# Low parts of forty weight units: an accumulating DMA in place of GpSimd's subtraction

## The chip, the cores and the metric

The kernel runs on one core of one Trainium2 chip. The metric is the device time of one execution in microseconds. Three runs of the kernel before took 841.36, 841.49 and 846.52 us; their median is 841.49.

The engines are named as the profile names them: PE is TensorE (PEld its weight loads), DVE is VectorE, ACT is ScalarE, POOL is GpSimd, SP is SyncE, which here only starts DMAs.

## The reference

Two layers of a decoder trunk work on 512 prompt rows and 8 sample rows of 1024 channels with shared weights. Layer 0 mixes two convolutions, layer 1 a gated unit over chunks of 128 rows. Cut to what matters here:

```python
def ab_mixer(x, ...):                       # layer 0
    z = x @ w_in                            # 1024 -> 7 x 1024
    a_val, a_gate, b_post, c_pre, h, g = split(z)
    a = causal_dwconv31(a_val * sigmoid(a_gate)) + bias
    a = silu(layer_norm(a))
    s = causal_dwconv3(c_pre * h)
    y = concat([a, b_post * s]) * silu(g)
    return y @ w_out                        # 2048 -> 1024

def c_mixer(x, ...):                        # layer 1
    u, v, g = split(x @ w_in)               # 1024 -> 3 x 2048
    u, v = gelu(u), layer_norm(gelu(v))
    mix = tril(w_s) @ v + b_s               # per chunk of 128 rows and head
    return (u * mix * silu(g)) @ w_out

x = layer_norm(alpha * x + mixer(x))        # after each layer
```

Everything is float32. The convolution states and the sample rows' v are outputs too.

## The kernel before

**Products in two parts.** The 520 rows are columns of every product, in two halves of 260; channels lie on the 128 partitions. The weights come as 136 units, numbered 0 to 135 in the order of their use. A unit holds 1024 input channels times 128 output channels, as a tile of 128 x 8 x 128 values (512 KB). TensorE multiplies in the type float32r, which keeps fewer bits than float32. So a weight tile `raw` is split into a high part `whi`, which is `raw` rounded to float32r, and a low part `wlo = raw - whi`; the rows are split likewise (`xh`, `xl`). A product is whi·xh + wlo·xh + whi·xl: 3 matmuls for each of 8 channel blocks and 2 halves, 48 to a unit (`mm2`).

**Where the parts come from.** `load_unit` (lines 116 to 125) does four things for unit n: SyncE starts the load into `raw` (3 buffers), ScalarE writes the high part by a cast (line 121), and the engine that `ON_POOL` (line 127) names subtracts for the low part (line 124): GpSimd for units 4 to 45 and 66 to 83, VectorE for the other 74. High and low parts lie in a ring of 12 tiles, so six units are there at a time and a unit's tiles can be filled once the unit six places ahead of it has been used. Units 0 and 1 are split in a start-up loop of their own. A unit is asked for `LEAD` = 5 units ahead.

**Layer 0.** Units 0 to 31 come in rounds of four for each of 8 channel blocks i: gate, value, c and h. ScalarE takes the sigmoid of the gate (`sg`), VectorE multiplies it with the value from PSUM (`apad`, line 306); ScalarE copies c, VectorE multiplies it with h from PSUM (`ch`, line 325). Two PSUM tiles (`zt`) serve these products in turn, so that a product can begin only when the one before the last has been emptied by ScalarE or VectorE. On VectorE also run the convolution of width 3 (`sB`, line 332, two steps a block) and that of width 31: 30 steps `acc` a block with the accumulator in PSUM (line 269), two blocks in turn, put in at low priority wherever the scheduler sees VectorE free. The sample rows' convolutions are `proda`, `cas`, `prodb`, `sbs`. Then come the units 32 to 39 (`z_post`, multiplied into sB by VectorE, line 392), 40 to 47 (gate of B), 48 to 55 (first half of the output projection), 56 to 63 (gate of A), and 64 to 71 (second half of the output projection, in two row halves, `out_part`), each followed by a layer norm over the channels whose steps are mostly VectorE's.

**Layer 1.** Units 72 to 87 give v, then u, gate and output projection in two rounds to unit 135.

**What sets the order.** Each engine works through its own queue in order. A scheduler with a model of the engines' times places the instructions in these queues when the kernel is built; so each engine's order is fixed in the program, and an instruction that waits holds all that stand behind it on its engine.

Of the kernel before, what the change touches and what calls it, by code (L numbers as in the profile page):

```python
# [9 lines left out]
F32 = mybir.dt.float32  # L10
# [3 lines left out]
ALU = mybir.AluOpType  # L14
# [3 lines left out]
D = 1024  # L18
# [12 lines left out]
ALPHA = 4.0 ** 0.25  # L31
EPS = 1e-5

# columns of the packed per-channel parameters
PA_W = 0
PA_B = 31
PA_G = 32
# [13 lines left out]
def decoder_kernel(  # L51
# [19 lines left out]
    nc = tc.nc  # L71
# [10 lines left out]
    def xs_slot(dt, name):  # L82
        return slots.tile([P, T], dt, tag="X", name=name, bufs=16)
# [25 lines left out]
    def hs(h):  # L109
        return slice(h * TH, (h + 1) * TH)  # L110

# [1 line left out]
    n_units = 2 + wu.shape[0]  # L113
    units = [None, None]

    def load_unit(wtag=("W", 12)):
        n = len(units)
        raw = wpool.tile([P, KT, P], F32, tag="raw", name=f"raw_{n}", bufs=3)
        nc.sync.dma_start(raw, wu[n - 2])
        hi = wpool.tile([P, KT, P], F32R, tag=wtag[0], name=f"whi_{n}", bufs=wtag[1])  # L120
        nc.scalar.copy(hi, raw)  # L121
        lo = wpool.tile([P, KT, P], F32R, tag=wtag[0], name=f"wlo_{n}", bufs=wtag[1])
        eng = nc.gpsimd if n in ON_POOL else nc.vector
        eng.tensor_tensor(lo, raw, hi.bitcast(F32), op=ALU.subtract)  # L124
        units.append((hi, lo))

    ON_POOL = set(range(4, 46)) | set(range(66, 84))
    EXTRA = set()
    for base in (64, 128):
        EXTRA.update((base + 6, base + 7))  # L130
# [31 lines left out]
                        stop=(k == KT - 1 and j == 2),  # L162
                    )

    # products of a constant until the first rows are there, so that the array's clock is up by then
    warm = const.tile([P, P], BF16, name="warm")
    nc.vector.memset(warm, 1.0)
    wps = mt("warm")
    for j in range(NWARM):
        nc.tensor.matmul(wps[:, :P], warm, warm, start=True, stop=True)  # L170

    # the input rows come with the first two weight units, one k tile after the other, and the
    # products follow in that order
    xh, xl = [], []
    w0h, w0l = [], []
    zg = zt("z_first")
# [2 lines left out]
    for k in range(KT):  # L179
        x = tmp(f"x_{k}")  # L180
        if k % 4 == 0:
            raw = wpool.tile([P, 4, 2, P], F32, tag="raw", name=f"raw_s{k}", bufs=3)
# [4 lines left out]
        cuts = 2 if k == 0 else 1  # L187
# [3 lines left out]
        h = xs_slot(F32R, f"xh_{k}")  # L191
        lo = xs_slot(F32R, f"xl_{k}")
# [22 lines left out]
    load_unit()  # L215
    pa = const.tile([P, KT, NPA], F32, name="pa")
    nc.sync.dma_start(pa, pa_in)
    # powers of two, so float32r holds them as well
    ones_r = const.tile([P, P], F32R, name="ones_r")
    ones_d = ones_r.bitcast(F32)  # L220
    nc.gpsimd.memset(ones_d, 1.0 / D)
# [6 lines left out]
    neg_half = const.tile([P, NS], F32, name="neg_half")  # L228
    nc.gpsimd.memset(neg_half, -0.5)

    # ================= layer 0 =================
    unit(1)
    xs = []
    for j in range(2):
        t = wpool.tile([P, 4, NS, WA], F32, tag="M", name=f"xs_{j}", bufs=4)
# [46 lines left out]
    n = 0  # L282
    for i in range(KT):
# [44 lines left out]
        s = slots.tile([P, T], F32, tag="SB", name=f"sB_{i}", bufs=8)  # L328
# [9 lines left out]
                op1=ALU.add,  # L338
            )

    # the sample rows of both convolutions
    nc.gpsimd.dma_start(cbs_out, xb)
    prodb = btmp("prodb")[:, : KT * NS * WB].rearrange("p (a b c) -> p a b c", a=KT, b=NS)
    nc.vector.tensor_tensor(
# [3 lines left out]
        op=ALU.mult,  # L348
# [5 lines left out]
    with background():  # L354
        for j in range(2):
# [6 lines left out]
                op=ALU.mult,  # L362
# [5 lines left out]
                    cA[i][:, SEQ:], cas[:, i - 4 * j, :], AF.Identity, bias=pa[:, i, PA_B : PA_B + 1]  # L368
                )

    # layer norm of the wide convolution over the channels, then silu
    def mean_of(m, src, name):
        """the sum of src / D over the channels, from its two float32r parts"""
        both = tpool.tile([P, T], F32R, tag="B", name=f"parts_{name}", bufs=4)
        nn = src.shape[-1]
        hi, lo = both[:, :nn], both[:, TH : TH + nn]
        nc.scalar.copy(hi, src)
        nc.vector.tensor_tensor(lo, src, hi.bitcast(F32), op=ALU.subtract)
        nc.tensor.matmul(m, ones_r, hi, start=True, stop=False)
        nc.tensor.matmul(m, ones_r, lo, start=False, stop=True)  # L380
# [11 lines left out]
        nc.vector.tensor_tensor(two(sB[i]), zh(z), two(sB[i]), op=ALU.mult)  # L392

    def split_y(i, g, other, tag, parts):
        """y = g * other as its two parts, in that many cuts of the rows"""
        h = y_slot(F32R, f"yh_{tag}{i}")
        lo = y_slot(F32R, f"yl_{tag}{i}")
        for j in range(parts):
            c = slice(j * T // parts, (j + 1) * T // parts)
            nc.vector.tensor_tensor(g[:, c], g[:, c], other[:, c], op=ALU.mult)  # L400
            nc.scalar.copy(h[:, c], g[:, c])
            nc.vector.tensor_tensor(lo[:, c], g[:, c], h[:, c].bitcast(F32), op=ALU.subtract)
        yh.append(h)
        yl.append(lo)
# [66 lines left out]
    gated(cA, "a")  # L471

    def out_part(base, c0, c1, yh, yl, res, lnc, done, last=False, pool_sub=()):
        """The second half of an output projection for the rows c0..c1, the residual, and the layer
        norm over the channels. The sums of the norm are of the rows less the mean of their first
        512 channels, so that no large mean cancels in the variance."""
        c = slice(c0, c1)
        nn = c1 - c0
        key = f"{base}_{c0}"
# [92 lines left out]
    def split_x1(d, c0, c1):  # L572
# [10 lines left out]
    out_part(n, TH, T, yh, yl, res, LN0_G, split_x1)()  # L583
    n += KT

    # ================= layer 1 =================
    wt = wpool.tile([P, NH, P], F32, tag="M", name="wt", bufs=4)
    nc.gpsimd.dma_start(wt, wsT_in)
    bs = wpool.tile([P, NH, P], F32, tag="M", name="bs", bufs=4)
    nc.gpsimd.dma_start(bs, bs_in)  # L590
    # wt[s, h, t] is kept where s <= t
    nc.gpsimd.affine_select(
        wt, wt, pattern=[[0, NH], [1, P]], compare_op=ALU.is_ge, fill=0.0, base=0, channel_multiplier=-1
    )
    # and its float32r parts, for the column sums
    wth, wtl = [], []
    for j in range(2):
        w = wt[:, 4 * j : 4 * j + 4, :].rearrange("p a b -> p (a b)")
# [29 lines left out]
    for i in range(NVF):  # L628
        z = one(i, f"z_v{i}_1")[:, :TH]
        mm(z, unit(n + i), x1h, x1l, hs(1))  # L630
        t = vt[i]
# [18 lines left out]
    def v_finish():  # L650
        v_tok(NV - 1)
        for c in range(NC):
            nc.vector.bn_aggr(mv[:, c, :], stats[:, c, :, :].rearrange("p a b -> p (a b)"))
        nc.vector.tensor_scalar_add(rs, mv[:, :, 1], EPS)
        nc.gpsimd.tensor_tensor(rs, rs, neg_half[:, :NC], op=ALU.pow)
        for i in range(NV):
            for c in range(NC):
                nc.vector.tensor_scalar(
                    vtok[i][:, c * P : (c + 1) * P],
                    vtok[i][:, c * P : (c + 1) * P],  # L660
                    mv[:, c, 0:1],
                    rs[:, c : c + 1],
                    op0=ALU.subtract,
                    op1=ALU.mult,
                )
        # column sums of the causal weights, for the shift of the norm
        for j in range(2):
            m = mt(f"rows_{j}")
            nc.tensor.matmul(m, ones_r, wth[j], start=True, stop=False)
            nc.tensor.matmul(m, ones_r, wtl[j], start=False, stop=True)  # L670
            nc.scalar.mul(
                rowsum[:, 4 * j : 4 * j + 4, :].rearrange("p a b -> p (a b)"), m, float(D)
            )
        # the sample rows' layer norm
        ssum = tiny.tile([P, NS], F32, name="ssum")
        nc.vector.tensor_reduce(ssum, vs.rearrange("p a b -> p b a"), axis=AX.X, op=ALU.add)
        m = mt("vs_mean")
        nc.tensor.matmul(m[:, :NS], ones_d, ssum, start=True, stop=True)
        smean = tiny.tile([P, NS], F32, name="smean")
        nc.vector.tensor_scalar_mul(smean, m[:, :NS], 0.5)  # L680
        bc = lambda t: t[:, None, :].to_broadcast([P, NV, NS])
        nc.vector.tensor_tensor(vs, vs, bc(smean), op=ALU.subtract)
        vq = mixs
        nc.vector.tensor_tensor(vq, vs, vs, op=ALU.mult)
        qsum = tiny.tile([P, NS], F32, name="qsum")
        nc.vector.tensor_reduce(qsum, vq.rearrange("p a b -> p b a"), axis=AX.X, op=ALU.add)
        m = mt("vs_var")
        nc.tensor.matmul(m[:, :NS], ones_d, qsum, start=True, stop=True)
        srs = tiny.tile([P, NS], F32, name="srs")
        nc.vector.tensor_scalar(srs, m[:, :NS], 0.5, EPS, op0=ALU.mult, op1=ALU.add)  # L690
        nc.gpsimd.tensor_tensor(srs, srs, neg_half, op=ALU.pow)
        nc.vector.tensor_tensor(vs, vs, bc(srs), op=ALU.mult)
        pb = lambda j: pv[:, :, j : j + 1].to_broadcast([P, NV, NS])
        nc.vector.tensor_tensor(vs, vs, pb(0), op=ALU.mult)
        nc.vector.tensor_tensor(vs, vs, pb(1), op=ALU.add)
        nc.gpsimd.dma_start(vs_out, vs)
        four = lambda t: t.rearrange("p (a c) b -> p a c b", c=2)
        nc.vector.tensor_tensor(
            four(mixs), four(vs), ws00[:, :, None, None].to_broadcast([P, NH, 2, NS]), op=ALU.mult
        )  # L700
        nc.vector.tensor_tensor(
            four(mixs), four(mixs), bs[:, :, None, 0:1].to_broadcast([P, NH, 2, NS]), op=ALU.add
        )
# [83 lines left out]


def _units(w, e0, e1):
    """[1024, e] columns e0..e1 as [n, 128 (k inside), 8 (k tile), 128]"""  # L790
    w = w[:, e0:e1]
    n = (e1 - e0) // P
    return w.reshape(KT, P, n, P).transpose(2, 1, 0, 3)


def _chan(a, n):
    """[..., n*128] -> [128, n, ...]"""
    a = a.reshape(a.shape[:-1] + (n, P))
    k = a.ndim
    return a.transpose((k - 1, k - 2) + tuple(range(k - 2)))  # L800
# [86 lines left out]
```

## Time and profile before

| | |
|---|---|
| runs | 841.36, 841.49, 846.52 us |
| profiled execution: span from its first to its last instruction | 840.8 us (its own time isn't listed beside it; the median lies 0.7 above the span) |
| mean granted TensorE clock | 0.991 |
| PE, DVE, ACT, POOL busy | 97%, 66%, 37%, 23% |
| GpSimd's subtractions for low parts | 60, 145.6 us |
| VectorE's subtractions for low parts | 74, 90.2 us |
| ScalarE's casts for high parts | 134, 140.0 us |
| read from HBM, written to it | 77.91 MB, 3.44 MB |

A busy share is an average over stages. VectorE is busy in nearly all of the first 250 us and less than two thirds of the time behind it; GpSimd's subtractions lie before 210 us and between 340 and 470 us. TensorE's matmuls overlap, so the count of matmuls in a stage tells more of its pace than its busy time: in an undisturbed stretch there are 355 in 42 us.

### The profile page before, as it was taken

The numbers are of one execution on the slowest core, as the hardware profiler recorded it, in microseconds if no ns is written. First come the engines' busy times: TensorE is split into PE (matmuls) and PEld (weight loads), VectorE is DVE, ScalarE is ACT, GpSimd is POOL, SyncE is SP. The second block draws the span as 40 slices with busy tenths as digits, with TensorE's granted clock in tenths as the row PEclk, the third lists the DMA queues.
The fourth block names the chain that finished last, engine by engine and source line by source line (L and its number), as shares of the span: only waits on it lengthen the run. The fifth ranks groups of instructions, "written<-read, shape, count | busy, mean of one in ns | idle before, by whom it ended". The sixth has DMA issues, their size and how long they took to land.

```text
span 840.8 us, 15982 instructions
## 1 busy us (share of the span) xinstructions
PE 816.4 (97%) x6792; PEld 813.8 (97%) x6792; DVE 557.8 (66%) x894; ACT 309.5 (37%) x470; POOL 193.7 (23%) x178
## 2 busy tenths in 40 slices
PE   9989999998999999999999999999999999999994
PEld 8989999998999999999999999999999999999993
DVE  5899999999994487356696333495455433625566
ACT  5423322333124346333466533333432133333243
POOL 0844355544340000024252711101000000000022
PEclk9999999999999999999999999999999999999998
DMA  8533333223223452424050522204223233222011
GB/s 301 164 103 101 101 103 102 96 82 130 72 79 101 122 166 66 126 76 126 26 166 12 171 81 82 95 24 156 77 76 95 82 101 94 83 79 99 1 51 51
DMA packets 27110, 82.38 MB, mean 98 GB/s; under 512 B 3568, under 2 KB 7296, under 8 KB 27040
## 3 DMA queue, kind: packets, MB, share of 16 engines
q1 hardware_dynamic: 26000, 79.01, 30.1%
q0 software_dynamic: 1040, 2.36, 0.7%
q8 instruction: 53, 0.87, 0.4%
q14 instruction: 17, 0.14, 0.1%
HBM read 77.91 MB, written 3.44 MB: 97 GB/s over the span
## 4 chain that ended last, share of the span: by engine, by line
PE 71%; DVE 23%; DMA 2%; issue 2%; ACT 1%; SPq 0%; POOL 0%; ACTq 0%; DVEq 0%; POOLq 0%
DVE acc L269 14%; PE z_gc L157 11%; PE z_u L157 11%; PE z_p L141 9%; PE z_v L157 7%; PE z_q L157 5%; PE z_o L157 5%; PE z_gb L157 5%; PE z_ga L157 5%; PE z_post L157 4%; PE z_v L141 4%; DVE sB L332 3%; DMA raw<-in_wu 2%; PE mix L713 2%; PE vt L615 1%
## 5 line engine op out<-in xcount | busy, mean ns | idle before, releaser
L121 ACT CAST whi<-raw 128x1024 fp32r<-128x1024 f32 x134 | 140.0, 1047 | 300.6 <-issue 66.6
L124 POOL TENSOR_TENSOR wlo<-raw,whi 128x1024 fp32r<-128x1024 f32 x60 | 145.6, 2434 | 262.6 <-ACT whi L121 262.3
L124 DVE TENSOR_TENSOR wlo<-raw,whi 128x1024 fp32r<-128x1024 f32 x74 | 90.2, 1222 | 131.0 <-ACT whi L121 131.0
L269 DVE SCALAR_TENSOR_TENSOR acc<-apad,pa,acc 128x512 f32<-128x512 f32 x240 | 166.6, 748 | 2.5 <-ACT acc L266 0.8
L157 PE MATMUL z_gc<-x1h,whi 128*128 128x260 f32 x256 | 72.9, 285 | 0.0
L157 PE MATMUL z_u<-x1h,whi 128*128 128x260 f32 x256 | 72.4, 283 | 0.0
L157 PE MATMUL z_gc<-x1h,wlo 128*128 128x260 f32 x256 | 72.0, 281 | 0.0
L157 PE MATMUL z_u<-x1l,whi 128*128 128x260 f32 x256 | 72.0, 281 | 0.0
L157 PE MATMUL z_gc<-x1l,whi 128*128 128x260 f32 x256 | 72.0, 281 | 0.0
L157 PE MATMUL z_u<-x1h,wlo 128*128 128x260 f32 x256 | 72.0, 281 | 0.0
L157 PEld LDWEIGHTS z_u<-x1h,wlo 128*128 128x128 f32 x256 | 48.1, 188 | 0.1
L157 PEld LDWEIGHTS z_gc<-x1h,wlo 128*128 128x128 f32 x256 | 48.2, 188 | 0.0
L157 PEld LDWEIGHTS z_u<-x1h,whi 128*128 128x128 f32 x256 | 48.1, 188 | 0.1
L157 PEld LDWEIGHTS z_gc<-x1l,whi 128*128 128x128 f32 x256 | 48.1, 188 | 0.0
L157 PEld LDWEIGHTS z_u<-x1l,whi 128*128 128x128 f32 x256 | 48.1, 188 | 0.0
L157 PEld LDWEIGHTS z_gc<-x1h,whi 128*128 128x128 f32 x256 | 48.1, 188 | 0.0
L725 POOL COPY mix<-mixs 128x8 f32<-128x8 f32 x16 | 3.5, 226 | 186.5 <-DVE gu L752 174.1
L157 PE MATMUL z_v<-x1h,whi 128*128 128x260 f32 x160 | 46.0, 287 | 0.0
L157 PE MATMUL z_v<-x1h,wlo 128*128 128x260 f32 x160 | 45.0, 281 | 0.0
L157 PE MATMUL z_v<-x1l,whi 128*128 128x260 f32 x160 | 44.9, 281 | 0.0
L157 PE MATMUL z_post<-xh,whi 128*128 128x260 f32 x128 | 36.8, 288 | 4.2 <-DVE sB L392 4.2
L157 PE MATMUL z_h<-xh,whi 128*128 128x260 f32 x128 | 36.9, 288 | 4.0 <-DVE apad L306 4.0
(259 smaller groups left out, 2758.5 us busy)
## 6 DMA issues: line engine op xcount, KB each, us to landing
raw<-in_wu SPq DMA_DIRECT2D x134, 512.0 KB, 3.6
xr<-in_xT SPq DMA_DIRECT2D x8, 260.0 KB, 4.6
x<-in_xT SPq DMA_DIRECT2D x7, 260.0 KB, 4.4
out_y<-r SPq DMA_DIRECT2D x8, 130.0 KB, 1.8
out_y<-out SPq DMA_DIRECT2D x4, 260.0 KB, 2.2
raw_s<-in_w SPq DMA_DIRECT2D x8, 128.0 KB, 4.2
xs<-in_cache_a SPq DMA_DIRECT2D x2, 496.0 KB, 9.2
out_cas<-xs POOLq DMA_DIRECT2D x2, 496.0 KB, 4.5
```

The source lines that it names most:

```text
L121: nc.scalar.copy(hi, raw)
L124: eng.tensor_tensor(lo, raw, hi.bitcast(F32), op=ALU.subtract)
L141: nc.tensor.matmul(ps, a[:, k, :], b[k][:, c], start=(k == 0 and j == 0), stop=(k == KT - 1 and j == 2),)
L157: nc.tensor.matmul(z[h][:, :TH], a[:, k, :], b[k][:, hs(h)], start=(k == 0 and j == 0), stop=(k == KT - 1 and j == 2),)
L269: nc.vector.scalar_tensor_tensor(acc[i], apads[i][:, j : j + SEQ], pa[:, i, PA_W + j : PA_W + j + 1], acc[i], op0=ALU.mult, op1=ALU.add,)
L332: nc.vector.scalar_tensor_tensor(s[:, :SEQ], ch[:, j : j + SEQ], pa[:, i, PB_W + j : PB_W + j + 1], s[:, :SEQ], op0=ALU.mult, op1=ALU.add,)
L615: nc.tensor.transpose(m[:, c * P : (c + 1) * P], vt[i][:, c * P : (c + 1) * P], ident)
L713: nc.tensor.matmul(m[:, c * P : (c + 1) * P], vtok[i][:, c * P : (c + 1) * P], wt[:, h, :], start=True, stop=True)
L725: nc.gpsimd.tensor_copy(t[:, SEQ:], mixs[:, i, :])
```

## The change

Units 10 to 49 get their low parts in another way. ScalarE, behind the cast for the high part, also writes `-raw` into the low part's tile, which is of the type float32r and so holds the negated high part. Then GpSimd starts a DMA that reads the same unit from HBM a second time and adds it to the tile in place: `-whi + raw`. GpSimd subtracts for no unit any more. Units 4 to 9 and 66 to 83, which it had besides, go to VectorE; units 46 to 49, which were VectorE's, are made by DMA. VectorE so makes the low parts of 94 loaded units in place of 74, and 40 DMAs of 512 KB are added, which read 21 MB more. Some comments go as well, which does nothing.

```diff
@@ load_unit
         hi = wpool.tile([P, KT, P], F32R, tag=wtag[0], name=f"whi_{n}", bufs=wtag[1])
         nc.scalar.copy(hi, raw)
         lo = wpool.tile([P, KT, P], F32R, tag=wtag[0], name=f"wlo_{n}", bufs=wtag[1])
-        eng = nc.gpsimd if n in ON_POOL else nc.vector
-        eng.tensor_tensor(lo, raw, hi.bitcast(F32), op=ALU.subtract)
+        if n in BY_DMA:
+
+            nc.scalar.mul(lo, raw, -1.0)
+            nc.gpsimd.dma_start(lo, wu[n - 2], accum_op=ALU.add)
+        else:
+            nc.vector.tensor_tensor(lo, raw, hi.bitcast(F32), op=ALU.subtract)
         units.append((hi, lo))
 
-    ON_POOL = set(range(4, 46)) | set(range(66, 84))
+
+    BY_DMA = set(range(10, 50))
     EXTRA = set()
```

## The prediction

> **What bounds the kernel now.** I read the page's busy shares first, then who waited for whom on TensorE, then the span cut into stages, then single instructions where TensorE stood still.
>
> The first line is from the page (busy us, share, instructions); the five below it are TensorE's waits (us in total, times, longest).
>
> ```profile
> PE 816.4 (97%) x6792; PEld 813.8 (97%) x6792; DVE 557.8 (66%) x894; ACT 309.5 (37%) x470; POOL 193.7 (23%) x178
> ...
> PE z_post L157 <- DVE sB L392: 4.2, 1, 4.2
> PE z_h L157 <- DVE apad L306: 4.0, 1, 4.0
> PE warm L170 <- DVE warm L167: 1.1, 1, 1.1
> PE shift L497 <- DVE tot L492: 0.8, 1, 0.8
> ...
> PE z_gate L157 <- ACT c L317: 0.6, 1, 0.6
> ```
>
> TensorE sets the time. The largest holes are two waits for VectorE, which must empty a PSUM tile before the next product may use it. The stages show the holes as missing matmuls (the number after x, first column group), with the granted clock (PEclk) beside them.
>
> ```profile
> 42.00:63.00 21.00, 17.00 (x130) 16.80 (x129) 20.72 (x29) 4.98 (x6) 10.03 (x8) 0.92 0.35 103
> 63.00:84.00 21.00, 21.00 (x179) 21.00 (x179) 20.75 (x28) 6.52 (x8) 9.56 (x6) 1.00 0.32 102
> 84.00:105.00 21.00, 20.36 (x172) 20.16 (x171) 20.93 (x26) 7.01 (x12) 8.22 (x9) 1.00 0.33 101
> 189.00:210.00 21.00, 18.77 (x158) 18.57 (x157) 20.96 (x29) 6.70 (x16) 9.83 (x9) 1.00 0.39 130
> 210.00:252.00 42.00, 40.02 (x325) 40.02 (x326) 40.38 (x52) 8.99 (x15) 16.88 (x7) 0.96 0.23 76
> 252.00:294.00 42.00, 42.00 (x355) 42.00 (x355) 18.28 (x22) 17.59 (x24) 0.00 (x0) 1.00 0.36 110
> 386.00:430.00 44.00, 42.48 (x349) 41.94 (x348) 32.93 (x62) 17.83 (x32) 15.26 (x7) 1.00 0.30 90
> ```
>
> A full stretch gives 355 matmuls in 42 us, 8.45 per us. Against that, 42–63 lacks 48, or 5.7 us; 84–105 lacks 6, or 0.7; 189–210 lacks 20, or 2.4; 210–252 lacks 30, or 3.5; 386–430 lacks 23, or 2.7. Each of the two waits of 4 us costs about 1.7 us more, since the clock is lower after it (0.08 of 21 us; 0.04 of 42). So 15.0 us can be had between the start and the tail, and no more: the floor is about 826.
>
> VectorE is late there because single instructions of it run long. The rows are VectorE's and GpSimd's timeline (start, duration), then four groups (count | busy us, mean ns), then two ranges (min/median/max ns).
>
> ```profile
> 36.37 7.68 DVE L332 SCALAR_TENSOR_TENSOR sB<-ch,pa,sB 128x512 f32<-128x512 f32 x1
> 36.37 7.13 POOL L124 TENSOR_TENSOR wlo<-raw,whi 128x1024 fp32r<-128x1024 f32 x3
> ...
> L332 DVE SCALAR_TENSOR_TENSOR sB<-ch,pa,sB 128x512 f32<-128x512 f32 x16 | 29.3, 1831 | 0.9 <-ACT sB L330 0.9
> L358 DVE TENSOR_TENSOR proda<-xs,pa 128x992 f32<-128x992 f32 x2 | 6.5, 3273 | 0.0
> L124 DVE TENSOR_TENSOR wlo<-raw,whi 128x1024 fp32r<-128x1024 f32 x74 | 90.2, 1222 | 131.0 <-ACT whi L121 131.0
> L124 POOL TENSOR_TENSOR wlo<-raw,whi 128x1024 fp32r<-128x1024 f32 x60 | 145.6, 2434 | 262.6 <-ACT whi L121 262.3
> ...
> L332 DVE SCALAR_TENSOR_TENSOR sB<-ch,pa,sB x16: 739/1154/7678, 33.4 to 207.1; 128x512 f32<-128x512 f32 x16
> L269 DVE SCALAR_TENSOR_TENSOR acc<-apad,pa,acc x240: 737/747/757, 23.4 to 247.5; 128x512 f32<-128x512 f32 x120
> ```
>
> The sB instruction that takes 0.74 us at best took 7.68 us and ended 0.55 us after three GpSimd subtractions of 7.13 us that began with it. The 240 conv steps, whose accumulator lies in PSUM, never stretch. So VectorE's instructions with two tensors in SBUF stand still while GpSimd subtracts. The 16 sB instructions lose 29.3 − 16 × 0.74 = 17.5 us so, the two proda ones 6.5 − 2 × 1.22 = 4.1 us (by the row of a slightly larger subtraction): 21.6 us before 210.
>
> **What the change costs and saves.** Three things move: 42 − 6 = 36 of GpSimd's first 42 subtractions and VectorE's four for units 46 to 49 become DMAs, 40 in all; units 4 to 9 and 66 to 83 go from GpSimd to VectorE, 24 × 1.22 = 29.3 us; ScalarE gets 40 negations.
>
> *The first wait, 42–63.* VectorE's order up to the product that empties unit 5's PSUM tile (apad_1), before:
>
> ```order
> L332 SCALAR_TENSOR_TENSOR sB_0_471<-ch_0_466,pa_296,sB_0_471 128x512
> L269 SCALAR_TENSOR_TENSOR acc_0_593<-apad_0_347,pa_296,acc_0_593 128x512
> L332 SCALAR_TENSOR_TENSOR sB_0_471<-ch_0_466,pa_296,sB_0_471 128x512
> L269 SCALAR_TENSOR_TENSOR acc_0_593<-apad_0_347,pa_296,acc_0_593 128x512 x8
> L306 TENSOR_TENSOR apad_1_587<-z_val1_532,sg_1_530 128x520
> ```
>
> and in the changed program (wlo_9 is the low part of unit 9):
>
> ```order
> L337 SCALAR_TENSOR_TENSOR sB_0_471<-ch_0_466,pa_296,sB_0_471 128x512
> L128 TENSOR_TENSOR wlo_9_480<-raw_9_476,whi_9_478 128x1024
> L274 SCALAR_TENSOR_TENSOR acc_0_594<-apad_0_347,pa_296,acc_0_594 128x512
> L337 SCALAR_TENSOR_TENSOR sB_0_471<-ch_0_466,pa_296,sB_0_471 128x512
> L274 SCALAR_TENSOR_TENSOR acc_0_594<-apad_0_347,pa_296,acc_0_594 128x512 x4
> L311 TENSOR_TENSOR apad_1_588<-z_val1_532,sg_1_530 128x520
> ```
>
> All six new subtractions stand ahead of apad_1, but the scheduler leaves 13 conv steps there instead of 20.
>
> ```profile
> 23.37 7.09 DVE L269 SCALAR_TENSOR_TENSOR acc<-apad,pa,acc 128x512 f32<-128x512 f32 x9 [0.81 <-ACT acc L266]
> ...
> 50.16 0.69 DVE L306 TENSOR_TENSOR apad<-z_val,sg 128x520 f32<-128x520 f32 x1
> ...
> 50.91 0.45 PE L157 MATMUL z_h<-xh,whi 128*128 128x260 f32 x1 [4.00 <-DVE apad L306]
> ...
> 31.71 1.05 ACT L121 CAST whi<-raw 128x1024 fp32r<-128x1024 f32 x1 [5.02 <-DMA raw<-in_wu]
> ```
>
> From 23.4: 13 × 0.79 (9 in 7.09) + 6 × 1.22 + 0.69 (ch) + 2 × 0.74 + 0.69 (apad) = 20.5, so 43.9; about 1 us more where VectorE comes to wlo_7 before its high part (31.71 + 1.05): 44.9. TensorE wants it at 50.91 − 4.00 = 46.9. Saved: 5.7 us, with 2 us to spare.
>
> *The second wait, 189–252.*
>
> ```profile
> 188.47 0.68 DVE L306 TENSOR_TENSOR apad<-z_val,sg 128x520 f32<-128x520 f32 x1
> 189.08 3.38 DVE L269 SCALAR_TENSOR_TENSOR acc<-apad,pa,acc 128x512 f32<-128x512 f32 x5
> ...
> 211.24 0.69 DVE L392 TENSOR_TENSOR sB<-z_post,sB 128x520 f32<-128x520 f32 x1
> ...
> L157 PE MATMUL z_post<-xh,wlo x128: 278/282/420, 196.3 to 247.4; 128*128 128x260 f32 x128
> ...
> 472.69 5.75 PE z_v L157 x48
> ```
>
> A unit takes TensorE 5.75 us. The first z_post product began at about 196.2 (its second matmul at 196.3), so apad_7's product had ended two units before, at 184.7; VectorE came to it 3.8 us late and needed 23.5 us to the end of L392, 211.9, where 207.7 (two units after 196.2) would have done. In the new order the work between them is 20 conv steps of 0.68, proda and its sum (1.2 + 1.1), four sB, tot_a and prodb and ch of 0.4 to 0.7 each, 19 to 20 us. Over a half round (two units, 11.5 us) the new order holds 13 to 15 conv steps, two sB every second time, and one or two products, 10 to 11.4 us; so without GpSimd's stretching VectorE isn't late at apad_7, and ends by 184.7 + 0.7 + 20 = 205.4. Saved: 2.4 + 3.5 = 5.9 us, and the 0.7 of 84–105, where ScalarE waited behind the same late VectorE.
>
> *The norm after layer 0, 386–470.* Behind the reciprocal VectorE's rows were
>
> ```order
> L533 RECIPROCAL rstd_64_0_4762<-rstd_64_0_4762 128x260
> L490 TENSOR_TENSOR tot_64_260_4874<-r_0_3479,r_1_3538 128x260
> L487 TENSOR_TENSOR r_2_3597<-z_p64_260_2_4876,r_2_3597 128x260
> L561 TENSOR_TENSOR r_0_3479<-r_0_3479,rstd_64_0_4762 128x260
> ```
>
> and are now, with the low parts of units 73 and 74 between them,
>
> ```order
> L538 RECIPROCAL rstd_64_0_4802<-rstd_64_0_4802 128x260
> L128 TENSOR_TENSOR wlo_73_4649<-raw_73_4645,whi_73_4647 128x1024
> L495 TENSOR_TENSOR tot_64_260_4914<-r_0_3519,r_1_3578 128x260
> L492 TENSOR_TENSOR r_2_3637<-z_p64_260_2_4916,r_2_3637 128x260
> L128 TENSOR_TENSOR wlo_74_4684<-raw_74_4680,whi_74_4682 128x1024
> L566 TENSOR_TENSOR r_0_3519<-r_0_3519,rstd_64_0_4802 128x260
> ```
>
> ```profile
> 387.18 5.08 DVE L400 TENSOR_TENSOR silu_a<-silu_a,cA 128x260 f32<-128x260 f32 x2
> 421.34 6.87 DVE L561 TENSOR_TENSOR r<-r,rstd 128x260 f32<-128x260 f32 x8
> ```
>
> Six subtractions come into this norm, 7.3 us, each able to wait at the head of VectorE's queue for ScalarE's high part while norm and evacuations stand behind it. What leaves is GpSimd's stretching: 6.87 − 8 × 0.42 = 3.5 us and 5.08 − 2 × 0.42 = 4.2 us. Bounds: a gain of the 2.7 us that 386–430 lacks, or a loss of the whole 7.3. I take a loss of 1, near the middle, as the two sums nearly cancel.
>
> *ScalarE and GpSimd.* The order of ScalarE had high part 10, the sigmoid, high part 11; now the negation follows the sigmoid:
>
> ```order
> L121 CAST whi_10_535<-raw_10_533 128x1024
> L296 ACTIVATE sg_1_530<-z_gate1_475 128x520
> L125 ACTIVATE wlo_10_537<-raw_10_533 128x1024
> L121 CAST whi_11_663<-raw_11_661 128x1024
> ```
>
> ```profile
> L121 ACT CAST whi<-raw 128x1024 fp32r<-128x1024 f32 x134 | 140.0, 1047 | 300.6 <-issue 66.6 <-PE z_u L157 44.9 <-PE z_q L157 34.4
> ```
>
> The 40 negations at 1.05 us are 42 us more on ScalarE, 1.05 in each 5.75, on an engine that is busy 4.98 of 21 us at 42–63. An evacuation behind one is 1.05 late where TensorE gives it 5.75: nothing, as long as VectorE is on time. GpSimd's small copies now stand between DMA issues, and a copy that waits for VectorE holds the next DMA.
>
> *The accumulating DMA.* The trace has none. What it has:
>
> ```profile
> q1 hardware_dynamic: 26000, 79.01, 30.1%
> ...
> raw<-in_wu SPq DMA_DIRECT2D x134, 512.0 KB, 3.6
> ...
> wt<-in_wsT POOLq DMA_DIRECT2D x1, 512.0 KB, 5.9
> bs<-in_bs POOLq DMA_DIRECT2D x1, 512.0 KB, 6.6
> ```
>
> A plain 512 KB takes the 16 engines 0.301 × 840.8 × 0.524 / 79.01 = 1.68 us, the low bound; the high bound is 6.6, if nothing overlaps. I take twice 1.68, 3.4 us, since each byte of the tile must be read too. With the unit's own load that is 5.0 us of each 5.75: it fits, narrowly. In latency it has room: a ring of 12 tiles lets a unit be filled five units, 28.7 us, ahead; ScalarE's 2.1 and a landing of 6.6 leave 20 us.
>
> The Trainium skill, "Collectives: The Full Stack", section "The bandwidth ceiling: the fold count and why AG ≠ RS ≠ AR", says that a reducing DMA runs at half a copy's rate because it reads two sources, and that the addition costs no cycles. By it the estimate would be 3.4 us as well, and by a plain copy's row 1.7; the sum is the same by both, and no run here shows it yet.
>
> The sum: 841.5 (the span, 840.8, and the 0.7 between it and the median) − 5.7 − 5.9 − 0.7 + 1.0 = 830.2; I say 830.
>
> **The rivals.** *New waits eat it.* If VectorE's place in the queue, not the stretching, makes one of the two waits, 5.9 come back; with 3 us lost in the norm, 838. For: VectorE is still full to 250 (40.38 of 42), and waits on ScalarE at wlo_7. Against: the 7.68 us and the 2 to 3 us margins above.
>
> *The DMA can't keep pace, and it is slower.* Place: units 10 to 49. If an accumulate takes the engines x us, TensorE loses 40 × (x + 1.68 − 5.75) less the 20 us of lead. It cancels the gain of 11 us from x = 4.85, and costs 1% from 5.05, three times a copy. At 5.5, 40 × 1.43 − 20 = 37, so 867; at 6.6, 40 × 2.53 − 20 = 81, so 911. For: nothing in the trace says how fast the addition is. Against: 3.4 needs only that it keeps up with reading.
>
> *Not what it says.* VectorE may be stretched by the DMAs' traffic as it was by GpSimd. In 42–84 loads move 100 GB/s and its conv steps stay at 737 to 757, so I give this no chance of its own; it would look like the first rival.
>
> **Numbers.** Forecast, 0.50: 826 to 833. New waits, 0.27: 833 to 850, within 1% or just beyond. The DMA, 0.23: 850 and up. One per cent is 8.4 us, about what can be told apart. Faster by over 1% (under 833.1): 0.50. Within 1%: 0.27. Slower: 0.23. The range is 826.5 to 858: a twentieth is left below, and above it the DMA rival from x = 5.3 on, 0.15.
>
> **What would show it.** Right: TensorE's waits for sB and apad gone, 355 matmuls in 42 us through 42–252, sB's maximum near 0.75 us, accumulates landing in under 20 us with TensorE never waiting for a DMA. Wrong: a TensorE wait that names the wlo DMA; a DMA share near 1 in 60–250; apad or sB waits still there with sB at 0.75; more than 4 us lacking in 386–470.

## The result and the profile after

The changed kernel takes 834.05 us (median of four runs, 832.82 to 834.73). The kernel before, on the same chip, takes 842.54 us. The ratio is 0.9889, with a 95% interval of 0.9865 to 0.9913. So it is faster by 1.1%, and 4 us above the forecast of 830. The profiled execution has a span of 833.0 us.

The busy shares on the page of the changed kernel:

```profile
PE 814.2 (98%) x6792; PEld 812.2 (98%) x6792; DVE 536.6 (64%) x914; ACT 347.2 (42%) x510; POOL 88.0 (11%) x158
```

TensorE's waits in the changed kernel (us in total, times, longest):

```profile
PE z_v L146 <- DVE r L492: 4.1, 1, 4.1
PE z_first L212 <- ACT xh L205: 1.2, 2, 1.0
...
PE z_c L162 <- DVE wlo L128: 0.3, 1, 0.3
```

The two waits of 4 us on `apad` and `sB` are gone. One wait of the same size is new: a `z_v` product waits for VectorE's evacuation `r`. The stages that the prediction used show the same as counts of matmuls:

```profile
42.00:63.00 21.00, 21.00 (x179) 21.00 (x178) 20.93 (x32) 9.33 (x12) 4.90 (x8) 1.00 0.92 206
84.00:105.00 21.00, 21.00 (x179) 21.00 (x178) 19.25 (x29) 10.11 (x15) 5.44 (x9) 1.00 0.93 208
189.00:210.00 21.00, 21.00 (x179) 21.00 (x179) 19.49 (x32) 10.91 (x20) 4.80 (x7) 1.00 0.90 202
210.00:252.00 42.00, 42.00 (x356) 42.00 (x355) 30.45 (x45) 19.20 (x23) 6.06 (x7) 1.00 0.86 181
386.00:430.00 44.00, 39.85 (x311) 39.55 (x310) 37.23 (x83) 22.24 (x44) 6.17 (x7) 0.93 0.31 96
```

Up to 252 us every stage is full and the granted clock is 1.00. The norm behind layer 0 now has 311 matmuls where 44 × 8.45 = 372 would fit: it lacks 61, or 7.2 us, and before it lacked 2.7. The sum closes on the profiled spans: 840.8 − 5.7 − 5.9 − 0.7 + (7.2 − 2.7) = 833.0.

VectorE's ranges (min/median/max ns) and the DMAs of the changed kernel (KB each, median us to landing; then queues: packets, MB, share of 16 engines):

```profile
L337 DVE SCALAR_TENSOR_TENSOR sB<-ch,pa,sB x16: 743/747/753, 35.7 to 195.3; 128x512 f32<-128x512 f32 x16
...
L311 DVE TENSOR_TENSOR apad<-z_val,sg x7: 690/700/701, 41.8 to 178.3; 128x520 f32<-128x520 f32 x7
```

```profile
q1 hardware_dynamic: 26000, 79.01, 32.2%
q0 software_dynamic: 6800, 23.33, 15.0%
...
raw<-in_wu SPq DMA_DIRECT2D x134, 512.0 KB, 3.9
wlo<-in_wu POOLq DMA_DIRECT2D x40, 512.0 KB, 7.7
```

No sB instruction takes more than 0.753 us; before, one took 7.68. The second `apad` starts at 41.8 and not at 50.16. GpSimd's queue had 0.7% of the 16 engines in the kernel before and has 15.0% now, so 40 accumulating DMAs take 0.143 × 833.0 = 119 us of all 16 engines, 2.98 each. A plain load is at 0.322 × 833.0 × 0.524 / 79.01 = 1.78.

### The profile page after: what moved, and what is told of

Same layout as the page of the kernel before. It is cut to its first block, busy times and chain, and to the rows that moved or that the text cites. A ratio compares the mean times of both kernels' runs of the same rounds, so it can differ in the third digit from the quotient of the medians.

```text
span 833.0 us, 16028 instructions
## 1 busy us (share of the span) xinstructions
PE 814.2 (98%) x6792; PEld 812.2 (98%) x6792; DVE 536.6 (64%) x914; ACT 347.2 (42%) x510; POOL 88.0 (11%) x158
## 3 DMA queue, kind: packets, MB, share of 16 engines
q1 hardware_dynamic: 26000, 79.01, 32.2%
q0 software_dynamic: 6800, 23.33, 15.0%
## 4 chain that ended last, share of the span: by engine, by line
PE 96%; DMA 1%; DVE 1%; ACT 0%; SPq 0%; issue 0%; ACTq 0%; DVEq 0%
PE z_p L146 11%; PE z_gc L162 11%; PE z_u L162 11%; PE z_v L162 7%; PE z_q L162 6%; PE z_o L162 6%; PE z_c L162 5%; PE z_ga L162 5%; PE z_post L162 5%; PE z_h L162 5%; PE z_gb L162 5%; PE z_val L162 5%; PE z_gate L162 5%; PE z_v L146 5%; PE mix L718 2%; PE vt L620 1%
## 5 line engine op out<-in xcount | busy, mean ns | idle before, releaser
L121 ACT CAST whi<-raw 128x1024 fp32r<-128x1024 f32 x134 | 139.9, 1048 | 324.9 <-PE z_u L162 44.9
L128 DVE TENSOR_TENSOR wlo<-raw,whi 128x1024 fp32r<-128x1024 f32 x94 | 114.4, 1224 | 142.5 <-ACT whi L121 141.9
L126 POOL DMA_DIRECT2D wlo<-in_wu x40 | 34.7, 869 | 139.2 <-ACT wlo L125 132.2
L125 ACT ACTIVATE wlo<-raw 128x1024 fp32r<-128x1024 f32 x40 | 42.2, 1055 | 0.0
L162 PE MATMUL z_c<-xh,wlo 128*128 128x260 f32 x128 | 36.1, 282 | 0.3 <-DVE wlo L128 0.3
L146 PE MATMUL z_p<-yh_c,whi 128*128 128x260 f32 x128 | 36.3, 284 | 0.0
```

The costliest lines, as they stand in the source:

```text
L125: nc.scalar.mul(lo, raw, -1.0)
L126: nc.gpsimd.dma_start(lo, wu[n - 2], accum_op=ALU.add)
L128: nc.vector.tensor_tensor(lo, raw, hi.bitcast(F32), op=ALU.subtract)
L146: nc.tensor.matmul(ps, a[:, k, :], b[k][:, c], start=(k == 0 and j == 0), stop=(k == KT - 1 and j == 2),)
L162: nc.tensor.matmul(z[h][:, :TH], a[:, k, :], b[k][:, hs(h)], start=(k == 0 and j == 0), stop=(k == KT - 1 and j == 2),)
```

## The experiments

All runs are beside the kernel before on the same chip, whose median was 842.7 to 843.6. "Lacks" means the matmuls that are missing against 8.45 per us. Unless a diff says otherwise, the edits are made in the changed kernel.

### Does GpSimd's reading stretch VectorE?

GpSimd makes one more subtraction for each of units 10 to 49, into the `raw` tile that nobody needs any more; the orders of the other engines stay as they are.

```diff
             nc.gpsimd.dma_start(lo, wu[n - 2], accum_op=ALU.add)
+            nc.gpsimd.tensor_tensor(raw, raw, hi.bitcast(F32), op=ALU.subtract)
```

> The changed kernel, with one more instruction for each of units 10 to 49: behind its DMA GpSimd subtracts the high part from the raw tile in place, for nothing. Every other engine's order is that of the changed kernel, row for row. If GpSimd's subtractions stretch VectorE's instructions with two tensors in SBUF (the theory), the sB instructions go from 0.747 us on average back to 1.2 to 1.9, VectorE is late by some us again, and waits of TensorE for apad, ch or sB come back: 2 to 10 us slower than the changed kernel, 836 to 844. If the gain came from VectorE's new order or from the smaller VectorE load (the rival), nothing else has changed and the time stays within 2 us of 834.

Measured: 861.68 us, ratio 1.0213 (1.0168 to 1.0259). TensorE's waits, then VectorE's groups (count | busy us, mean ns), then stages, then GpSimd's and VectorE's timeline of this run:

```profile
PE z_h L163 <- DVE apad L312: 8.6, 4, 3.6
PE z_post L163 <- DVE ch L331: 5.7, 1, 5.7
PE z_post L163 <- DVE sB L398: 5.6, 1, 5.6
```

```profile
L338 DVE SCALAR_TENSOR_TENSOR sB<-ch,pa,sB 128x512 f32<-128x512 f32 x16 | 35.6, 2222 | 0.0
L364 DVE TENSOR_TENSOR proda<-xs,pa 128x992 f32<-128x992 f32 x2 | 11.9, 5970 | 0.0
```

```profile
42.00:63.00 21.00, 21.00 (x179) 21.00 (x179) 20.93 (x28) 9.17 (x12) 13.93 (x13) 1.00 0.89 196
105.00:126.00 21.00, 17.41 (x133) 17.20 (x132) 20.96 (x24) 7.01 (x10) 12.48 (x9) 0.92 0.70 149
...
189.00:210.00 21.00, 18.39 (x153) 17.99 (x151) 21.00 (x19) 6.86 (x9) 9.25 (x8) 1.00 0.72 177
210.00:252.00 42.00, 32.89 (x236) 32.69 (x237) 40.76 (x55) 12.83 (x23) 20.53 (x15) 0.84 0.59 131
```

```profile
197.56 2.75 POOL L127 TENSOR_TENSOR raw<-raw,whi 128x1024 f32<-128x1024 f32 x1
199.90 0.92 POOL L362 DMA_DIRECT2D out_cas<-xs  x1
200.51 1.21 POOL L126 DMA_DIRECT2D wlo<-in_wu  x1
201.08 3.05 POOL L127 TENSOR_TENSOR raw<-raw,whi 128x1024 f32<-128x1024 f32 x1
```

```profile
197.31 7.88 DVE L364 TENSOR_TENSOR proda<-xs,pa 128x992 f32<-128x992 f32 x1
```

Waits for `apad` and `sB` are back, though nothing in VectorE's order has changed. The ones for `apad` end at 118.9, 144.7, 171.2 and 196.1 us, the one for `ch` at 213.5 and the one for `sB` at 227.4. Where the first old wait stood, at 50.9 us, none came: 42–63 is full, since the added subtractions begin at 39.8 us and stretch nothing before 42. So this run shows that the stretch alone makes TensorE wait; it does not try the first wait. A `proda` of 1.19 us takes 7.88, through two subtractions and the DMA issues between them. The effect was far larger than expected: VectorE's instructions lost 33.3 us before 210 us by the measure of the table further below, and a lowered clock (0.84 in one row) came on top of the waits.

In the next run GpSimd is busy there as well, but reads nothing:

```diff
             nc.gpsimd.dma_start(lo, wu[n - 2], accum_op=ALU.add)
+            for _ in range(2):
+                nc.gpsimd.memset(raw, 0.0)
```

> As the run with the idle subtraction, but GpSimd instead sets the raw tile of each of units 10 to 49 to zero, twice, behind the unit's DMA: about 2 us of GpSimd that writes the same tile and holds the raw buffer as long, and reads no tensor. All other engines keep the order of the changed kernel. If what stretched VectorE there was GpSimd reading (theory), sB stays at 0.75 us and the time at 834 within 2. If it was GpSimd being busy, or the raw buffer held longer, the loss of that run (27 us) comes back for most of its size: over 850.

Measured: 834.14 us, the changed kernel's time. sB and GpSimd's memsets in this run:

```profile
L339 DVE SCALAR_TENSOR_TENSOR sB<-ch,pa,sB x16: 740/744/747, 35.1 to 195.2; 128x512 f32<-128x512 f32 x16
```

```profile
L128 POOL MEMSET raw<- 128x1024 f32 x80 | 90.4, 1130 | 2.1
```

With 90.4 us of GpSimd's writing beside it, sB stays at 0.744 us; 11 of the 16 sB and both `proda` overlap a memset. So it is GpSimd's reading that stops VectorE's instructions with two tensors in SBUF, not its being busy, its writing, or a `raw` tile held longer. The Trainium skill, "SBUF — State Buffer", section "Who interferes with whom", says the same: such an instruction of VectorE contends with a GpSimd instruction that reads SBUF and not with one that only writes it. These two runs agree.

### Is the DMA needed?

In these and the later kernels with `ON_POOL`, the line that subtracts picks GpSimd for the units in it and VectorE for the rest. In the first kernel VectorE subtracts for every unit; in the second GpSimd subtracts for 10 to 45 as in the kernel before, and VectorE for the others. No DMA accumulates in either.

```diff
-    BY_DMA = set(range(10, 50))
+    BY_DMA = set()
+    ON_POOL = set()                    # first kernel
+    ON_POOL = set(range(10, 46))       # second kernel
```

> No DMA and no GpSimd: VectorE subtracts for all units, 40 x 1.22 = 49 us more of it by 260 than in the changed kernel, where it idles some 25 us by 252. Theory: nothing is stretched, but VectorE is full; what the scheduler can't push behind 252 makes TensorE wait, 836 to 850. If it is faster than 834, the DMA was not needed at all, only GpSimd's silence.

> The changed kernel without its DMAs: GpSimd subtracts for units 10 to 45, VectorE for all others (4 to 9, 46 to 49, 66 to 83 too). TensorE's order is that of the changed kernel. Theory: VectorE is stretched again by 15 us or more before 210, so the second wait is back, and the late wait of 4.1 us stays: 838 to 846, as slow as before or slower. Rival (the gain lies in where 4 to 9 and 66 to 83 went): 834.

Measured: 834.22 us (ratio 0.9892, 0.9865 to 0.9920) and 833.83 us (0.9887, 0.9857 to 0.9918). Both have the gain of the changed kernel without its DMA, and in both the theory missed. Where VectorE subtracts for all, it is full for longer (210 to 252 us in this row), yet TensorE lacks nothing, since conv steps that nobody waits for move back (the last begins at 305.1 us, in the changed kernel at 239.0):

```profile
210.00:252.00 42.00, 42.00 (x355) 42.00 (x355) 40.03 (x56) 14.08 (x19) 0.00 (x0) 1.00 0.34 101
```

Where GpSimd subtracts for 10 to 45, the 16 sB and the two `proda` took:

```profile
L339 DVE SCALAR_TENSOR_TENSOR sB<-ch,pa,sB 128x512 f32<-128x512 f32 x16 | 15.9, 994 | 0.0
L365 DVE TENSOR_TENSOR proda<-xs,pa 128x992 f32<-128x992 f32 x2 | 2.4, 1188 | 0.9 <-POOL xs L314 0.9
```

The sB lose 15.9 − 16 × 0.743 = 4.0 us, in the kernel before 17.5, with 36 of the same 42 subtractions on GpSimd. So the prediction's cause is right as a mechanism, but the loss isn't a fixed price of each subtraction: it depends on which instruction of VectorE stands beside which subtraction.

### Which part of the change takes which wait away?

Two kernels each undo one half of what the change does to GpSimd before 250 us. In the first GpSimd has 4 to 9 again and the DMA has 10 to 49; in the second, the other way round, GpSimd has 10 to 45 as before and only 4 to 9 have moved to VectorE. In both GpSimd has 66 to 83, as before.

```diff
+    BY_DMA = set(range(10, 50));  ON_POOL = set(range(4, 10)) | set(range(66, 84))    # first
+    BY_DMA = set();               ON_POOL = set(range(10, 46)) | set(range(66, 84))   # second
```

> The changed kernel with two groups of units given back to GpSimd: 4 to 9, and 66 to 83 (the second as in the run at 830.5 us, beside which this one is read); units 10 to 49 stay with the accumulating DMA. With 4 to 9 off VectorE its program has again 20 convolution steps ahead of the second padded tile, as in the kernel before. Theory A (the first wait is made by those 20 steps, and by GpSimd's six subtractions that stretch them): a wait of 3 to 5 us for the padded tile at 47 to 52 us and its clock loss of 1.7 us come back, the second wait near 210 us does not: 834 to 837 us. Rival B (the order is no cause; what stretched the instructions were the subtractions of units 10 to 45): no wait there, 830.5 us, within 1. Rival C (both waits come back): 840 or more.

> The kernel before with one edit: GpSimd no longer subtracts for units 4 to 9, VectorE does. Units 10 to 45 and 66 to 83 stay with GpSimd; no DMA accumulates, ScalarE negates nothing. Theory A (what the change gains is the order of VectorE's program after 4 to 9 have moved to it; the DMA is not needed): both waits gone, and the wait at 424 us of the changed kernel does not come, since GpSimd has 72 to 77: 830 to 831 us. Rival B (as the prediction had it: GpSimd's subtractions for 10 to 45 stretch VectorE's steps and make the second wait, whatever the order): the first wait gone only, 836 to 837 us. Rival C (4 to 9 were not the cause at all): 842 us.

Measured: 830.83 us (0.9853, 0.9821 to 0.9885) and 831.59 us (0.9859, 0.9831 to 0.9887). Half of the change, either half, is enough for the gain: the kernel with all of it and the same units 66 to 83 on GpSimd (run a below) takes 830.51. The first kernel, with 20 conv steps ahead of the second padded tile as before, in TensorE's waits, in the stages and on VectorE's and GpSimd's timeline:

```profile
PE z_h L164 <- DVE apad L313: 1.8, 1, 1.8
```

```profile
42.00:63.00 21.00, 19.16 (x161) 18.96 (x161) 20.71 (x31) 10.76 (x13) 4.08 (x7) 1.00 0.90 205
```

```profile
35.79 5.33 DVE L339 SCALAR_TENSOR_TENSOR sB<-ch,pa,sB 128x512 f32<-128x512 f32 x1
```

```profile
35.80 4.77 POOL L129 TENSOR_TENSOR wlo<-raw,whi 128x1024 fp32r<-128x1024 f32 x2
```

Two subtractions in a row stretch this sB to 5.33 us, where three made it 7.68, and the wait is 1.8 us instead of 4.0: 2.2 us less wait for 2.35 less stretch. By its time this run went to rival B, but by its trace to theory A at less than half its size; the wait of 1.8 us also cost no clock (1.00). The second kernel, in TensorE's waits and in VectorE's groups:

```profile
PE z_post L164 <- DVE sB L399: 0.3, 1, 0.3
```

```profile
L339 DVE SCALAR_TENSOR_TENSOR sB<-ch,pa,sB 128x512 f32<-128x512 f32 x16 | 17.4, 1088 | 0.0
```

Of the second wait 0.3 us is left, with GpSimd subtracting right through it. The table sums, from the traces, how far VectorE's instructions that start before 210 us exceed the median of the same operation and tile in the run where VectorE subtracts for all (excesses above 0.15 us):

| kernel | GpSimd's units before 250 us | stretch before 42 us | 42 to 210 us | apad, sB waits |
|---|---|---|---|---|
| before | 4–45 | 8.6 | 14.3 | 4.0, 4.2 |
| 4 to 9 on GpSimd | 4–9 | 6.2 | 0 | 1.8, none |
| 4 to 9 on VectorE | 10–45 | 1.6 | 5.9 | none, 0.3 |
| GpSimd 10 to 45 only | 10–45 | 0 | 6.0 | none, 0.3 |
| changed | none | 0 | 0 | none, none |

The first wait follows the stretch before 42 us, the second that behind it. When only units 4 to 9 leave GpSimd, the stretch before 210 us by the 36 that stay falls from about 16.6 us (14.3, and 2.35 for the third of the three subtractions beside the sB of 7.68, which was unit 10's) to 1.6 + 5.9 = 7.5. The starts show how. An sB that is stopped ends 0.55 us after the subtraction beside it, so it loses little but what is left of that subtraction. Behind 42 us, six sB begin 0.1 to 1.8 us into a subtraction of 2.4 in the kernel before and lose 0.8 to 2.1 us each; in the kernel with 4 to 9 on VectorE six begin 1.2 to 1.9 us into one and lose 0.3 to 1.1. Why the new order puts them later is not settled.

The table ends at 210 us, the subtractions don't: in the kernel before, the last seven of GpSimd's first 42 begin between 211 and 249 us, where the section on the profile before has none. They stretch `tot_a` by another 5.3 us (1.7 with 10 to 45 on GpSimd), and no product waits there after 212 us.

### What the new wait costs

In the changed kernel VectorE has the subtractions of units 72 to 77 within the norm. Its timeline there (rows in between are left out):

```profile
400.68 1.23 DVE L128 TENSOR_TENSOR wlo<-raw,whi 128x1024 fp32r<-128x1024 f32 x1 [0.53 <-ACT whi L121]
...
407.10 1.17 DVE L128 TENSOR_TENSOR wlo<-raw,whi 128x1024 fp32r<-128x1024 f32 x1
...
408.85 1.22 DVE L128 TENSOR_TENSOR wlo<-raw,whi 128x1024 fp32r<-128x1024 f32 x1
...
413.37 2.37 DVE L128 TENSOR_TENSOR wlo<-raw,whi 128x1024 fp32r<-128x1024 f32 x2
...
417.75 1.22 DVE L128 TENSOR_TENSOR wlo<-raw,whi 128x1024 fp32r<-128x1024 f32 x1 [0.51 <-PE z_p L146]
...
421.83 1.76 DVE L504 TENSOR_TENSOR r<-r,shift 128x260 f32<-128x260 f32 x5
...
424.27 0.75 DVE L492 TENSOR_TENSOR r<-z_p,r 128x260 f32<-128x260 f32 x2
```

Six subtractions, 7.2 us, stand in the queue ahead of the two evacuations at 424.27, and the product that needs their PSUM tile begins at 424.83 after 4.15 us of waiting. Five runs move these units elsewhere:

```diff
+    BY_DMA = set(range(10, 50));                       ON_POOL = set(range(66, 84))  # a
+    BY_DMA = set(range(10, 50)) | set(range(66, 84));  ON_POOL = set()               # b
+    BY_DMA = set(range(10, 50)) | set(range(72, 78))                                 # c
+    BY_DMA = set(range(72, 78));                       ON_POOL = set()               # d
+    BY_DMA = set();                                    ON_POOL = set(range(72, 78))  # e
```

Run a:

> The changed kernel with units 66 to 83 back on GpSimd as before; units 10 to 49 still by DMA, 4 to 9 by VectorE. If VectorE's own subtractions make the new wait of 4.1 us at 424 (theory), that wait goes and the stage 373 to 430 lacks about 2.7 us as before instead of 7.2: 828 to 831. If the wait comes from where the scheduler put the shift product, it may stay: 834.

Run b:

> The changed kernel with units 66 to 83 also by negation and accumulating DMA, so that neither GpSimd nor VectorE subtracts for them. Theory: the wait at 424 goes, no stretching comes in its place, and the stage lacks 0 to 3 us: 826 to 830. Rival: ScalarE, which has casts and activations of the norm in that stage, gets 18 negations of 1.05 us and takes VectorE's place as the late one: 832 to 838.

Run c:

> The changed kernel with units 72 to 77 by negation and DMA as well, which are the six whose subtractions stand in VectorE's order inside the norm; 66 to 71 and 78 to 83 stay on VectorE. Theory: these six alone make the wait at 424, which goes, and no DMA is waited for, since the other twelve aren't loaded twice: 827 to 830, below the runs with all of 66 to 83 on GpSimd or by DMA. Rival: it is the shift product's place in TensorE's order, or the other twelve: 832 to 835.

Run d:

> VectorE subtracts for all units but 72 to 77, which the accumulating DMA makes; GpSimd none. It is the run in which VectorE subtracts for all (834.2 us) with these six taken off it. Theory: of the gain the DMA is needed for none before 300 us, and the wait of 3.7 us at 424 us goes with the six units: 828 to 831 us, 190 MB less traffic in 16 engine shares than in the run at 827.3 us notwithstanding. Rival (VectorE is too full without the DMA for 10 to 49, and the convolution runs late into the norm): no gain, 834 us.

(The 190 MB in the text of d is a slip: 40 DMAs of 0.524 MB are 21 MB.)

Run e:

> VectorE subtracts for all units but 72 to 77, which GpSimd makes; no DMA accumulates. It is the run before this one of the same call with the six units on GpSimd. Theory: GpSimd's six subtractions stretch VectorE's instructions in the norm (the group of eight at the norm's end took 6.87 us each in the kernel before and 2.81 in the changed one), but VectorE has room there once six units are off it: 829 to 831 us, 1 to 2 us above the same with the DMA. Rival (the stretch costs as much as the six subtractions did): the wait at 424 us stays, 833 to 834 us.

(The 6.87 and 2.81 us in the text of e are for the whole group of eight, not for each.)

| run | 72 to 77 on | us | ratio (95%) | matmuls in 373–430, of 482 |
|---|---|---|---|---|
| changed | VectorE | 834.05 | 0.9889 (0.9865–0.9913) | 420 |
| VectorE for all | VectorE | 834.22 | 0.9892 (0.9865–0.9920) | 425 |
| a | GpSimd, with 66–71 and 78–83 | 830.51 | 0.9861 (0.9846–0.9875) | 459 |
| b | DMA, with 66–71 and 78–83 | 832.63 | 0.9899 (0.9858–0.9941) | 450 |
| c | DMA | 827.27 | 0.9811 (0.9785–0.9836) | 475 |
| d | DMA | 827.96 | 0.9815 (0.9788–0.9843) | 474 |
| e | GpSimd | 829.51 | 0.9838 (0.9805–0.9872) | 466 |

The wait at 424 us is absent in all five. Taking just the six units off VectorE is worth 834.05 − 827.27 = 6.8 us with the DMA for 10 to 49 and 834.22 − 827.96 = 6.3 without it; the matmuls gained, 55 and 49, are 6.5 and 5.8 us. Runs c and d differ by 40 DMAs and not in their ratio, which shows again that the DMA for 10 to 49 does nothing for the time. On GpSimd the six units are worth somewhat less (e: 466 matmuls, not 474, and 829.5 us). Run b found a new wait, in TensorE's waits:

```profile
PE z_p L148 <- DMA wlo<-in_wu: 2.8, 1, 2.8
```

There a product had to wait for an accumulating DMA, and the run's times scatter from 829.95 to 837.17. Runs c and d beat both kernels: 1.9% below the kernel before, with all stages full to 386 us in d and no wait above 1.1 us.

### How near is the DMA to its limit?

Each `raw` of units 10 to 49 is loaded twice, so that a unit moves three times 512 KB.

```diff
         nc.sync.dma_start(raw, wu[n - 2])
+        if n in BY_DMA:
+            nc.sync.dma_start(raw, wu[n - 2])
```

> The changed kernel, with the plain load of each of units 10 to 49 made twice into the same tile, the second behind the first. All other engines keep their order. Accumulate and two loads then ask for about 3.0 + 1.8 + 1.8 = 6.6 us of the 16 DMA engines in each 5.75 us. If the DMA's pace is a bound close by (the rival that was priced by 40 times the excess less 20 us of lead), TensorE loses 40 x 0.85 - 20 = 14 us, 848, with waits for wlo or whi. If the DMA share of 0.9 is mostly packets that queue behind each other and not work, the time stays within 2 us of 834.

Measured: 887.89 us, ratio 1.0537 (1.0486 to 1.0589). TensorE's waits, ScalarE's wait and two rows of its timeline, and four stages:

```profile
PE z_c L164 <- ACT sg L298: 10.4, 3, 4.7
PE z_gate L164 <- ACT c L324: 8.6, 2, 5.2
PE z_gb L164 <- DVE sB L399: 5.1, 1, 5.1
```

```profile
ACT whi L123 <- DMA raw<-in_wu: 163.6, 44, 9.3
```

```profile
90.06 1.05 ACT L123 CAST whi<-raw 128x1024 fp32r<-128x1024 f32 x1 [6.96 <-DMA raw<-in_wu]
91.01 0.60 ACT L298 ACTIVATE sg<-z_gate 128x520 f32<-128x520 f32 x1
```

```profile
42.00:105.00 63.00, 58.34 (x479) 58.14 (x478) 52.24 (x78) 28.52 (x37) 13.82 (x22) 0.97 0.93 246
105.00:189.00 84.00, 72.92 (x575) 72.11 (x573) 64.79 (x98) 30.41 (x37) 14.15 (x23) 0.94 0.85 221
189.00:252.00 63.00, 53.25 (x406) 52.65 (x407) 45.62 (x70) 22.50 (x37) 10.25 (x16) 0.92 0.86 220
252.00:315.00 63.00, 53.73 (x417) 53.36 (x417) 28.97 (x43) 26.41 (x33) 8.69 (x10) 0.92 0.88 232
```

By the changed kernel's rows a unit now needs 2.98 + 2 × 1.78 = 6.54 us of the 16 engines, and TensorE uses one in 5.75. That is 40 × 0.79 = 31.6 us short, and TensorE's idle time in these four stages is 273 − 238.2 = 34.8 us. The match is looser than it looks: this run's own queues (99.98 MB in 35.2% and 23.33 MB in 14.0% of 883.0 us) give 1.63 us for a load and 2.94 for an accumulating DMA, 6.2 in all, which is 18 us short. How much of the idle time is lack of pace and how much is loads that come late one by one stays open. The stages lack 273 × 8.45 − 1877 = 430 matmuls, 50.9 us; so the lowered clock accounts for the other 16.1. The 20 us of lead that the prediction took off were not there. The traces show why: ScalarE's cast waits at the head of its queue for a load, and the evacuations `sg` and `c` stand behind it, so TensorE waits for an evacuation and not for a weight tile: the `sg` at 91.01 stood behind a cast that had waited 6.96 us, and the product that needed its PSUM tile began at 91.66 after 4.66 us. Not every late load does this; ScalarE waited 163.6 us for loads in all, and TensorE was idle for 34.8.

## Why the prediction was right, and where it was not

**Right, to the size, up to 252 us.** Every stage from 42 to 252 us is full, as foretold: the 5.7, 5.9 and 0.7 us came in whole, the lowered clock among them. sB is at 0.75 us, and `apad` begins at 41.8 us, earlier than the 43.9 to 44.9 that the step gave for its end. For the second wait the step gave 0.7 + 20 us from `apad_7` to the end of the first sB product; it is 20.9 (178.3 to 199.2).

**The cause of the two waits.** GpSimd's reading stretches VectorE's instructions, and adding it back alone, with every order kept, brings waits for `apad` and `sB` back, though not the first one at its place. For the first wait the step argued by order, 13 conv steps in place of 20. No run has 20 steps without stretch, or 13 with the old stretch. The kernel with 4 to 9 on GpSimd has the 20 steps: there the wait shrank by about what the stretch shrank, and as 6.2 us of stretch were left against a wait of 1.8, we estimate that it would go if the stretch went, whatever the order. For the second wait the step gave an end at 205.4 where 207.7 was enough, 2.3 us of room. The kernel with 4 to 9 on VectorE has 2.6 us of stretch behind 189 us (0.6 on sB, 1.3 and 0.7 on `tot_a`), and waits 0.3 us: the size of the room was about right.

**What it left unsaid.** The 21.6 us of stretch were put to GpSimd's subtractions as a whole, as if all had to go (and left out `prodb`'s 1.3). Taking 6 of the 42 off, or the other 36, gave the gain as well.

**The wrong step: the norm.** The step "I take a loss of 1, near the middle, as the two sums nearly cancel" is the term that was mis-sized; it measured 4.5 us (7.2 lacking, less 2.7), within its bounds of −2.7 and 7.3. The stretching did go (the group of eight at line 566 takes 2.81 us, where it took 6.87). But sums of VectorE's work were the wrong scale: what sets the wait is what stands ahead of the one evacuation that TensorE needs next, and there six subtractions of 7.2 us had come in. With 4.5 in place of 1.0 the sum gives 833.7, and 834.05 was measured. A little of the agreement is luck: the sum starts from 841.5, and beside the result the kernel before took 842.54, from which the forecast would have been 831.2 and the mended sum 834.7. The measured time lies just above 826 to 833, which had 0.50, in the range of the first rival; as a ratio it is just over the 1% for which 0.50 was given as well. The prediction named the sign of it: "more than 4 us lacking in 386–470".

**The accumulating DMA.** Estimated at 3.4 us of the 16 engines, it took 2.98, 1.7 times a plain load of 1.78. The place of the slower rival was right, but its price had 20 us of lead in it. Without the lead the pace is lost from 5.75 − 1.78 = 3.97 us on, 1.0 us above what was measured, and a gain of 11 us is cancelled from 3.97 + 11/40 = 4.25 on, not from 4.85. That rival was so nearer than its price said. This is an estimate from the run with two loads; no run slows the accumulating DMA itself. The sign "a DMA share near 1" came close, at 0.86 to 0.93, and nothing was lost. The Trainium skill, "Collectives: The Full Stack", section "The bandwidth ceiling: the fold count and why AG ≠ RS ≠ AR", says of a reduce-scatter that it runs at half an all-gather's rate, because its addition reads two sources. A plain load of 1.78 us doubled would be 3.56; the measured 2.98 is somewhat better than that. ScalarE's 42.2 us of negations cost nothing that any wait shows.

**The first rival**, new waits that eat the gain, came true in small, at another place: one wait in the norm, not one of the two old ones.

**The rival with no chance of its own**, stretching by the DMAs' traffic, was set aside because the conv steps stay at 737 to 757 ns. That could not show it, as GpSimd doesn't stretch these steps either. The result does: sB stays at 743 to 753 ns with 181 to 208 GB/s beside it.

## What to carry to other kernels

When one engine's instructions run long beside another's, find the few that are hit and the wait that they lengthen; moving a handful of the offenders can be worth as much as removing all. When work moves to an engine that is half idle on average, look in each stage at what it will stand ahead of in that engine's queue, and price it by the wait of whoever needs the next result. Slack in buffers is no slack in time when an in-order engine waits for the late item at the head of its queue.

## What was not expected of the hardware

- A short head start protected some instructions of VectorE and not others. An sB that began 0.32 us ahead of a subtraction took its 0.74 us, and the subtraction took 2.70 us in place of 2.4; so it was in the kernel before at 111.64, 0.22 us ahead (0.74 and 2.77). The rows are of the kernel with 10 to 45 on GpSimd:

```profile
38.40 0.74 DVE L339 SCALAR_TENSOR_TENSOR sB<-ch,pa,sB 128x512 f32<-128x512 f32 x1
38.72 2.70 POOL L129 TENSOR_TENSOR wlo<-raw,whi 128x1024 fp32r<-128x1024 f32 x1 [4.39 <-ACT whi L121]
```

- But `proda` at 197.31, 0.25 us ahead of a subtraction at 197.56, took 7.88 us and went on through the next subtraction, 0.77 us after the first; in the kernel before one that began 0.20 us ahead took 3.68. The Trainium skill, "SBUF — State Buffer", section "Who interferes with whom", says that the order of issue decides which of the two engines blocks. The two sB agree with that; the two `proda` do not by their start times, though the profile calls spans on GpSimd rough.
- The stretch before 210 us by the same 36 subtractions ranged from 6.0 to about 16.6 us with VectorE's order, and 40 of them added beside an otherwise unchanged program cost 27.6 us of the kernel's time (861.68 − 834.05).
- An accumulating DMA of 512 KB into SBUF took 1.7 times the engine time of a plain load, and landed after 7.7 us where a plain load took 3.9. With a DMA share of 0.86 to 0.93 from 42 to 252 us no product waited for it.
